# Turning blocks 1 to 7 of the first two x tiles ahead of the first gate product, in a new order of the opening

## The chip, the core and the metric

The kernel runs on one core of a Trainium2 chip. The metric is the device time of one execution in microseconds, lower is better. Before the change three runs gave 669.2, 669.93 and 670.37 us, a median of 669.93 us.

The core's engines each run their own list of instructions in order and meet only at semaphores: TensorE (PE, with weight loads shown as PEld), VectorE (DVE), ScalarE (ACT), GpSimd (POOL) and SyncE (SP, which here only issues DMAs). ScalarE can issue DMAs too, on a queue of its own.

## The reference, cut to what matters

The reference is one step of a hybrid diffusion backbone layer over nine tiles of 128 tokens (one tile of prompt, eight of latent tokens), 1024 features wide. Of it the change touches only the front of the first of these lines:

```
shift, scale, gate = modulation(cond, w_mod, b_mod)          # silu(cond) @ w_mod + b_mod
h = rmsnorm(x, norm_gain) * (1.0 + scale) + shift
q_a, k_a, v_a, g_a, q_b, k_b, v_b, g_b = project(h, w_in)     # columns of one product h @ w_in
o = attention over all keys (group A) and over a band (group B)
y = x + gate * (concat(o_a * silu(g_a), o_b * silu(g_b)) @ w_out)
```

All of it is in float32. The kernel splits each operand of a large product into a high and a low part and makes three products of them (high by high, low by high, high by low).

## The kernel before, in words

The program begins with an *opening* that makes `h`, turned so that features lie on partitions, and beside it the first gate products `g_a` (a product of the 512 columns of `w_in` that make the gates of group A). It ends with the kernel's third piece of tokens, in the loop `gates(W_GA, 0, W_QA, THIRDS[2:])`. The rest of the kernel (the other projections, the attention, the output product) isn't touched by the change.

**The data.** `x` comes in nine tiles `xn0` to `xn8` of 128 tokens by 1024 features (`load_x`, 512 KB each; tile 0 is the prompt and comes last). The modulation weights come in eight pieces `wm0` to `wm7` (`load_wm`, 1 MB each), of which three fit at a time; the gate weights in eight pieces `rawga_0` to `rawga_7` (`W_GA.load`, 256 KB each), of which three fit. A small identity matrix (`ident`, 64 KB) and a table of columns (`colt`, 24 KB: the conditioning vectors, the norm gain, the bias) are loaded first. All of these loads are issued by SP in one queue.

**The steps.** For a feature block `j` (0 to 7), the opening makes these:

- `norm(t)`: for a tile of x, the sum of squares on ScalarE (L594; with `halves` one half of it on VectorE, L597) and the root on GpSimd (L601, L599, L603); `scaled(t)` multiplies the tile by it in place (L587 on VectorE, L585 on ScalarE).
- `modulate_rows(j)`: eight products (shown as sixteen instructions in the trace) of the silu of the condition with `wm[j]` on TensorE (L551, into `pm`), and a copy to `mrows` on VectorE (L556). I call this *rows j*.
- `modulate(j)`: two transposes of `mrows` (L562) and three small instructions on VectorE, which give the scale `a_mod` and the shift `b_col` of block j (L568 to L572).
- `transposed(j, t0, n)`: turns block j of n tiles from t0 on into a PSUM bank `px` on TensorE (L608, one transpose of 128x128 for each tile), applies scale and shift on ScalarE (L617, into `hf`), makes the high part of h on VectorE (L622) and the low part on GpSimd (L623).
- `W_GA.split`: high part of the weights on ScalarE (L435), low part on VectorE (L440), and the load of the next piece on SP.
- `first_half(half, parts)`: the gate products of block 0, for tiles 1 and 2 (half 0) and for tiles 3 and 4 (half 1) apart (L648, 128x256 each). `first_gates(ch, k)`: the products of block k for tiles 1 to 4 (L467, L468, L463, 128x512 each), into four PSUM banks `big`. `next_gates(ch, k)`: those of tiles 5 and 6 (128x256 each), into two banks `small`.
- `warm(n)`: n products of the identity by itself (L631) whose result nobody reads.

**The order.** The order of the opening's instructions on each engine is the order in which the program calls these steps. Before, it stands in a loop over j with a dozen conditions and small tables (`TURNED`, `BEHIND`, `WARM`, `LOADS`, `PAIRED`): 16 warm-up products, rows 0, block 0 of tiles 1 and 2 turned, six more warm-up products around `modulate(0)`, and then the first gate product; from there on four transposes (tiles 1 to 4) for each further block j, just ahead of its gate products. The modulation of blocks 4 and 5 and of 6 and 7 is made in pairs.

PSUM has eight banks: four `big`, two `small`, and two (`D` and `E`) that take turns for `pm` and `px`.

Of the kernel before, what the change touches and what calls it, by code (L numbers as in the profile page):

```python
# [20 lines left out]
P = 128  # L21
# [29 lines left out]
X_FROM = 2  # L51
SECOND_FROM = 5
LOADS = (1, 2, "m", 3, 4, "w", "m", "w", "m", 5, 6)
WARM = (16, 1, 5)
FULL = 1
MROWS_ACT = (7,)
SOON = 8
PAIRED = (4, 6)

TURNED = ((), (), (), (0,), (1, 2), (3,), (4, 5), (6, 7), (), ())  # L60
BEHIND = ((), (), (), (), (0,), (1, 2), (3,), (4, 5), (6,), (7,))
WIDE = 5
# [237 lines left out]
def hybrid_step(ctx, tc, x_prompt, x_sample, cache_k_a, cache_v_a, cache_k_b, cache_v_b,  # L300
# [104 lines left out]
    class Weights:  # L405
# [32 lines left out]
        def low(self, k, h, l):  # L438
            eng = nc.gpsimd if self.tag in POOL_LO and k % 2 else nc.vector
            eng.tensor_tensor(l, self.raw[k], h, op=ALU.subtract)  # L440
            self.hi.append(h)
            self.lo.append(l)
            self.load()
# [73 lines left out]
    with tc.tile_pool(name="st", bufs=2, side="right") as st:  # L517
        ident = st.tile([P, P], F32, name="ident", bufs=1)
        nc.sync.dma_start(ident, k_ident)
# [3 lines left out]
        nc.sync.dma_start(colt, cols)  # L523
        st.tile([P, 16], F32, name="pad3", bufs=1)

        wm = []

# [46 lines left out]
        xn = {}  # L574

        def load_x(t):
            xn[t] = st.tile([P, D], F32, name=f"xn{t}", bufs=1)
# [28 lines left out]
        def turned(px, j, t0, n):  # L606
            for i in range(n):
                nc.tensor.transpose(px[:, P * i : P * i + P], xn[t0 + i][:, P * j : P * j + P], ident)  # L608

        def transposed(j, t0, n, cond, px=None):  # L610
            if px is None:
                px = bank_tr(f"px{j}_{t0}")
                turned(px, j, t0, n)
# [3 lines left out]
            nc.scalar.activation(hf[:, :w], px[:, :w], AF.Identity,  # L617
                                 scale=a_mod[:, j, cond : cond + 1], bias=b_col[:, j, cond : cond + 1])
# [5 lines left out]

        for step in LOADS:
            load_x(step) if step in FIRST else W_GA.load() if step == "w" else load_wm(len(wm))

# [4 lines left out]

        rest = [7, 8, 0]
        second = [(j, 7, 2, 0) for j in range(WIDE)] + [(j, 0, 1, 1) for j in range(KT)]

# [19 lines left out]
        def more():  # L655
            ready = [x for x in second if x[0] <= j]
            if ready and j >= SECOND_FROM:
                second.remove(ready[0])
                transposed(*ready[0])

        for j in range(KT + 2):
            if j == 0:
                for t in (1, 2):
                    norm(t)
                    scaled(t)
                warm(WARM[0])
                modulate_rows(0)
                turned(small[1], 0, 1, 2)
                warm(WARM[1])
                modulate(0)  # L670
                warm(WARM[2])
                norm(3)
                norm(4, True)
                scaled(3, slice(0, 2 * P))
                transposed(0, 1, 2, 0, small[1])
                hi = W_GA.high()
                scaled(4, slice(0, 2 * P), nc.scalar)
                W_GA.low(*hi)
                first_half(0, 0)
                transposed(0, 3, 2, 0)  # L680
                modulate_rows(1)
                first_half(0, 1, 2)
                load_wm(3)
                continue
            if j == 1:
                modulate(1)
                W_GA.split()
                transposed(1, 1, 4, 0)
                first_half(1, 0, 1, 2)
                scaled(3, slice(2 * P, D))  # L690
                scaled(4, slice(2 * P, D), nc.scalar)
                load_wm(4)
                norm(5)
                continue
            big_on, behind = j <= KT, BEHIND[j]
            if SOON <= j < KT:
# [943 lines left out]
```

## Time and profile before

| | before |
|---|---|
| time, median of three runs | 669.93 us |
| the profiled execution's time | 669.37 us |
| span of the profiled execution, first to last instruction | 667.5 us |
| TensorE busy, share of the span | 98% |
| VectorE, ScalarE, GpSimd busy | 66%, 42%, 50% |
| chain of work that ended last: share on TensorE | 92% |
| first gate product starts | 14.78 us |
| product of the opening's last stretch (`pg`, after the last turn) starts | 66.90 us |

The profiled execution took 1.87 us more than its span, and 0.56 us less than the median of the three runs. In the lines of a timeline the columns are the start in us, the length in us, the engine, the source line, the operation, what it writes and reads, its size and how many of them are merged; in brackets is how long the engine had been idle before, and what let it go. In a table of windows each engine has its busy time and its number of instructions; the last three columns are the granted clock of TensorE, the mean busy share of the 16 DMA engines and the GB/s that they moved. A chain is read in order of time: start, length, what it was spent on.

### The profile page before, as it was taken

The numbers are of one execution on the slowest core, as the hardware profiler recorded it, in microseconds if no ns is written. First come the engines' busy times: TensorE is split into PE (matmuls) and PEld (weight loads), VectorE is DVE, ScalarE is ACT, GpSimd is POOL, SyncE is SP. The second block draws the span as 40 slices with busy tenths as digits, with TensorE's granted clock in tenths as the row PEclk, the third lists the DMA queues.
The fourth block names the chain that finished last, engine by engine and source line by source line (L and its number), as shares of the span: only waits on it lengthen the run. The fifth ranks groups of instructions, "written<-read, shape, count | busy, mean of one in ns | idle before, by whom it ended". The sixth has DMA issues, their size and how long they took to land.

```text
span 667.5 us, 10648 instructions
## 1 busy us (share of the span) xinstructions
PE 655.5 (98%) x3757; PEld 517.5 (78%) x3757; DVE 438.6 (66%) x924; ACT 281.3 (42%) x586; POOL 332.3 (50%) x324
## 2 busy tenths in 40 slices
PE   6999999999999999999999999999999999999997
PEld 2789988887788788997777777777777777777766
DVE  3566147786684766446768878688787786875533
ACT  4555411242142453435554355444454355434531
POOL 2457013332321232357885575657665675557712
PEclk9999999999999999999999999999999999999999
DMA  8980365437645211744142302223132212332233
GB/s 323 413 304 6 131 231 151 91 77 224 185 108 146 91 48 37 224 127 148 56 132 100 99 31 97 89 72 96 41 119 88 72 53 83 124 92 78 76 103 111
DMA packets 55837, 81.41 MB, mean 122 GB/s; under 512 B 7388, under 2 KB 26932, under 8 KB 54760
## 3 DMA queue, kind: packets, MB, share of 16 engines
q1 hardware_dynamic: 47752, 69.06, 30.9%
q10 hardware_dynamic: 8032, 11.68, 6.9%
q8 instruction: 30, 0.49, 0.3%
q14 instruction: 23, 0.19, 0.1%
HBM read 61.42 MB, written 19.29 MB: 121 GB/s over the span
## 4 chain that ended last, share of the span: by engine, by line
PE 92%; DVE 2%; ACT 2%; DMA 2%; issue 1%; ACTq 1%; SPq 0%; POOL 0%; DVEq 0%
PE pv L1432 15%; PE po L1507 15%; PE st L1390 7%; PE st L1391 7%; PE pmx L1130 5%; PE pq L454 4%; PE pq L455 4%; PE pq L453 4%; PE pg L468 3%; PE pg L463 3%; PE pg L467 3%; PE pk L454 2%; PE pk L455 2%; PE pk L453 2%; PE pmx L1133 2%; DMA xn<-in_x_sample_dram 1%
## 5 line engine op out<-in xcount | busy, mean ns | idle before, releaser
L1415 POOL TENSOR_TENSOR acc<-acc,pe 128x512 f32<-128x512 f32 x112 | 150.0, 1339 | 6.8 <-ACT pe L1402 0.6
L1402 ACT ACTIVATE pe<-st 128x512 f32<-128x512 f32 x208 | 120.4, 594 | 65.0 <-PE st L1391 52.3
L1143 DVE TENSOR_REDUCE mx<-pmx 128x1 f32<-128x384 f32 x192 | 104.4, 553 | 34.9 <-PE pmx L1130 32.1
L1432 PE MATMUL pv<-pe,v_all 128*64 128x256 f32 x832 | 96.8, 381 | 0.0
L1432 PEld LDWEIGHTS pv<-pe,v_all 128*64 128x64 f32 x832 | 58.3, 137 | 33.0 <-PE st L1391 4.2
L1507 PE MATMUL po<-wo,ogh 128*128 128x512 f32 (+1 forms) x224 | 79.5, 387 | 0.0
L372 POOL TENSOR_TENSOR rs_q<-ms_q,mhalf 128x8 f32<-128x8 f32 x18 | 34.8, 1931 | 80.1 <-DVE ms_q L370 80.1
L1130 PE MATMUL pmx<-kha,qt 128*128 128x384 f32 x192 | 64.1, 347 | 0.0
L1390 PE MATMUL st<-qt,kha 128*128 128x512 f32 x144 | 57.4, 398 | 0.5 <-ACT pe L1402 0.5
L1391 PE MATMUL st<-qb,kla 65*128 65x512 f32 x144 | 57.1, 396 | 0.0
L1148 DVE CUSTOM_DVE_ANT_0 pmx<-pmx,mask,nsink 128x512 f32<-128x512 f32 (+1 forms) x64 | 44.2, 722 | 11.4 <-PE pmx L1133 11.4
L1507 PEld LDWEIGHTS po<-wo,ogh 128*128 128x128 f32 x224 | 41.6, 189 | 9.5 <-ACT ogh L1469 0.6
L1464 POOL TENSOR_TENSOR spare<-spare,sgl 128x256 f32<-128x256 f32 x27 | 19.5, 735 | 50.0 <-DVE spare L1460 47.5
L1130 PEld LDWEIGHTS pmx<-kha,qt 128*128 128x128 f32 x192 | 35.3, 189 | 11.4 <-issue 5.0
L1507 PE MATMUL po<-wo,ogl 128*128 128x512 f32 (+1 forms) x112 | 43.2, 386 | 0.0
L1415 DVE TENSOR_TENSOR acc<-acc,pe 128x512 f32<-128x512 f32 x28 | 34.3, 1226 | 5.2 <-ACT pe L1402 3.9
L623 POOL TENSOR_TENSOR h<-hf,h 128x256 fp32r<-128x256 f32 (+2 forms) x33 | 28.0, 864 | 19.2 <-DVE h L622 19.2
L861 ACT ACTIVATE sqq<-pq 128x512 f32<-128x512 f32 x18 | 10.8, 599 | 53.6 <-DMA qd<-qo0q 15.7
L1390 PEld LDWEIGHTS st<-qt,kha 128*128 128x128 f32 x144 | 27.2, 189 | 5.7 <-ACT pe L1402 1.2
L467 PE MATMUL pg<-h,whigb 128*128 128x512 f32 (+2 forms) x88 | 30.0, 341 | 0.0
L1391 PEld LDWEIGHTS st<-qb,kla 65*128 65x128 f32 x144 | 27.0, 188 | 3.5
L468 PE MATMUL pg<-h,wlogb 128*128 128x512 f32 (+2 forms) x88 | 29.7, 337 | 0.0
(231 smaller groups left out, 1495.4 us busy)
## 6 DMA issues: line engine op xcount, KB each, us to landing
qt<-qd SPq DMA_DIRECT2D x36, 256.0 KB
wm<-in_w_mod_ss_dram SPq DMA_DIRECT2D x8, 1024.0 KB
qd<-qo0q ACTq DMA_DIRECT2D x36, 128.0 KB
qd<-qo1q ACTq DMA_DIRECT2D x36, 128.0 KB
qb<-qd SPq DMA_DIRECT2D x36, 128.0 KB
sgl<-gd SPq DMA_DIRECT2D x36, 128.0 KB
out_dram<-yt SPq DMA_DIRECT2D x17, 256.0 KB
xn<-in_x_sample_dram SPq DMA_DIRECT2D x8, 512.0 KB
```

What stands on the lines that cost most here:

```text
L453: nc.tensor.matmul(out, h_at(0, i, k, tok), w.hi[k], start=(k == 0), stop=False)
L467: nc.tensor.matmul(out, w.hi[k][:, cs], h_at(0, i, k, to), start=(k == 0 and first), stop=False)
L468: nc.tensor.matmul(out, w.lo[k][:, cs], h_at(0, i, k, to), start=False, stop=False)
L1130: nc.tensor.matmul(pm[:, 0:384], lhs, kha[:, g, 3 * b : 3 * b + 3, :], start=True, stop=True)
L1143: nc.vector.tensor_reduce(mx[:, h, b : b + 1], pm[:, 0:384], axis=AX.X, op=ALU.max)
L1148: nc.vector.tensor_tensor_reduce(s, s, mask[:, m0 : m0 + P * (p1_ - p0)], -1.0, nsink[:, 4 * g + h : 4 * g + h + 1], op0=ALU.add, op1=ALU.min,
L1390: nc.tensor.matmul(s, kh, qtile[i], start=True, stop=False)
L1391: nc.tensor.matmul(s, kl, qbtile[i], start=False, stop=True)
L1402: nc.scalar.activation(pe, v["s"], AF.Exp)
L1415: (nc.vector if (m, b) in ADD_DVE else nc.gpsimd).tensor_tensor(acc[i], first, pe, op=ALU.add)
L1432: nc.tensor.matmul(pv[HD * s : HD * s + HD, o : o + 256].rearrange("p (c n) -> p c n", c=2), lhs, r[:, :, s, :], start=start, stop=stop)
L1507: nc.tensor.matmul(po[c], x, wo_parts[KT * n + k][lo][:, q], start=(k == KS[0] and p == 0), stop=(k == KS[-1] and p == 2))
```

## The change

1. The loop over j, its tables and the `LOADS` list are replaced by one written table `OPENING`, a list of steps in the order in which they are called, each of them one of the functions above or a part of one. `W_GA` no longer loads its next piece by itself after a split; the table says when.
2. Tiles 1 to 4 of x lie in one buffer `x14` instead of four buffers of their own. Tile 2 is loaded and normed ahead of tile 1.
3. The loads of `ident` and `colt` are issued on ScalarE's queue instead of SP's.
4. Blocks 1 to 7 of tiles 1 and 2 are turned ahead of the first gate product (`early`, 14 transposes into the four `big` banks, which are empty then) and copied back to their place in `x14` (`kept`: two pairs of blocks on ScalarE, a pair and a single block on VectorE). Later, `turned` leaves these out, and `transposed` applies scale and shift with two instructions of 128x256 on ScalarE, one from `x14`, one from the bank with tiles 3 and 4, where one of 128x512 stood.
5. The warm-up products are 16 at the start and 14 ahead of the first gate product, where 16, 1 and 5 stood.
6. The order of the rest is new too: which gate products stand between which turns, and some of the scaling moves from one engine to another (`scaled(2)` and `scaled(7)` to ScalarE, the first columns of tile 4 to VectorE; tiles 1, 6 and 0 are normed in halves on two engines).

```diff
+OPENING = (('x', 2), ('x', 1), ('wm',), ('x', 3), ('x', 4), ('w',), ('wm',), ('w',), ('norm', 2), ('wm',),
+           ('norm', 1, True), ('scaled', 1, 0, 8, False), ('x', 6), ('warm', 16), ('x', 5),
+           ('scaled', 2, 0, 8, True), ('turn', 0, 1, 2, True), ('early', 1, 3, 2, 1), ('rows', 0),
...
-        nc.sync.dma_start(ident, k_ident)
+        nc.scalar.dma_start(ident, k_ident)
...
-        nc.sync.dma_start(colt, cols)
+        nc.scalar.dma_start(colt, cols)
...
+        x14 = st.tile([P, 4, D], F32, name="x14", bufs=1)
...
-            xn[t] = st.tile([P, D], F32, name=f"xn{t}", bufs=1)
+            xn[t] = x14[:, t - 1] if 1 <= t <= 4 else st.tile([P, D], F32, name=f"xn{t}", bufs=1)
...
             for i in range(n):
+                if (j, t0 + i - (t0 + i + 1) % 2) in own:
+                    continue
                 nc.tensor.transpose(px[:, P * i : P * i + P], xn[t0 + i][:, P * j : P * j + P], ident)
...
-            nc.scalar.activation(hf[:, :w], px[:, :w], AF.Identity,
-                                 scale=a_mod[:, j, cond : cond + 1], bias=b_col[:, j, cond : cond + 1])
+            for i in range(0, n, 2 if (j, t0) in own or (j, t0 + 2) in own else n):
+                at = slice(P * i, w if n < 2 or (j, t0) not in own and (j, t0 + 2) not in own else P * i + 2 * P)
+                if (j, t0 + i) in own:
+                    out = hf[:, at].rearrange("p (t c) -> p t c", c=P)
+                    x = x14[:, t0 + i - 1 : t0 + i + 1, P * j : P * j + P]
+                else:
+                    out, x = hf[:, at], px[:, at]
+                nc.scalar.activation(out, x, AF.Identity,
+                                     scale=a_mod[:, j, cond : cond + 1], bias=b_col[:, j, cond : cond + 1])
...
+        def early(b, j0, n, t0):
+            at[b] = big[b] if b < 4 else small[0] if b == 4 else bank_tr(f"pe{b}")
+            for i in range(n):
+                for k in range(2):
+                    nc.tensor.transpose(at[b][:, P * (2 * i + k) : P * (2 * i + k) + P],
+                                        xn[t0 + k][:, P * (j0 + i) : P * (j0 + i) + P], ident)
+
+        def kept(b, j0, n, t0, on_act=False):
+            (nc.scalar.copy if on_act else nc.vector.tensor_copy)(
+                x14[:, t0 - 1 : t0 + 1, P * j0 : P * (j0 + n)].rearrange("p t (j c) -> p j t c", c=P),
+                at[b][:, 0 : 2 * P * n].rearrange("p (j t c) -> p j t c", t=2, c=P))
+            own.update((j0 + i, t0) for i in range(n))
...
+        for name, *args in OPENING:
+            act[name](*args)
```

What this does to the order on the engines is shown at three places. Names carry a running number at their end; `x14` is the buffer of tiles 1 to 4, `pg0_1_f` to `pg0_3_f` are `big` banks.

SP's queue at the start of the program, before (the loads of `ident` and `colt`, then tiles 1 and 2, then the modulation weights):

```order
L519 DMA ident_163<-in_k_ident_dram 128x128
L523 DMA colt_167<-in_cols_dram 128x48
L578 DMA xn1_177<-in_x_sample_dram 128x1024
L578 DMA xn2_179<-in_x_sample_dram 128x1024
L530 DMA wm0_181<-in_w_mod_ss_dram 128x2048
L578 DMA xn3_183<-in_x_sample_dram 128x1024
```

and after:

```order
L616 DMA x14_177<-in_x_sample_dram 128x1024 x2
L567 DMA wm0_186<-in_w_mod_ss_dram 128x2048
L616 DMA x14_177<-in_x_sample_dram 128x1024 x2
L450 DMA rawga_0_190<-in_w_in_dram 128x512
L567 DMA wm1_192<-in_w_mod_ss_dram 128x2048
```

The two small loads no longer stand ahead of the first tile in SP's queue; the rest of this queue keeps nearly its order (tile 6 ahead of tile 5, two gate pieces a place earlier). ScalarE's list at the same place, before (the sums of squares L594 of tiles 1 to 4, then scale and shift L617 of block 0, then the high part of the first weights L435):

```order
L594 ACTIVATE sq1_205,ss1_206<-xn1_177 128x1024
L594 ACTIVATE sq2_213,ss2_214<-xn2_179 128x1024
L594 ACTIVATE sq3_262,ss3_263<-xn3_183 128x1024
L594 ACTIVATE sq4_269,ss4_270<-xn4_185 128x512
L617 ACTIVATE hf0_1_278<-pg0_2_s_204,b_col_151,a_mod_150 128x256
L435 CAST whiga_0_282<-rawga_0_187 128x512
```

and after:

```order
L632 ACTIVATE sq2_196,ss2_197<-x14_177 128x1024
L632 ACTIVATE sq1_205,ss1_206<-x14_177 128x512
L623 ACTIVATE x14_177<-x14_177,rsx2_201 128x1024
L718 COPY x14_177<-pg0_1_f_179 128x2x2x128
L718 COPY x14_177<-pg0_2_f_180 128x2x2x128
L632 ACTIVATE sq3_272,ss3_273<-x14_177 128x1024
L632 ACTIVATE sq4_279,ss4_280<-x14_177 128x512
L661 ACTIVATE hf0_1_301<-pg0_2_s_183,b_col_151,a_mod_150 128x256
L465 CAST whiga_0_305<-rawga_0_190 128x512
```

Three instructions now stand between the sums of squares of the first two tiles and that of tile 3: the scaling of tile 2 and two of the four copies back. TensorE's list from rows 0 on, before (rows 0 is `pm0<-wm0`; `px` and `pg0_2_s` take turned blocks):

```order
L551 MATMUL pm0_237<-wm0_181,sil32_174 32x256 x8
L608 MATMUL pg0_2_s_204<-ident_163,xn1_177 128x128
L608 MATMUL pg0_2_s_204<-ident_163,xn2_179 128x128
L631 LDWEIGHTS ident_b_103
L631 MATMUL pg0_0_s_203<-ident_b_103 128x512
L562 MATMUL pm0_237<-ident_163,mrows0_246 128x128 x2
```

and after, from the end of the first 16 warm-up products on:

```order
L648 MATMUL pg0_2_s_183<-ident_163,x14_177 128x128 x2
L714 MATMUL pg0_1_f_179<-ident_163,x14_177 128x128 x4
L588 MATMUL pm0_241<-wm0_186,sil32_174 32x256 x8
L714 MATMUL pg0_0_f_178<-ident_163,x14_177 128x128 x4
L714 MATMUL pg0_2_f_180<-ident_163,x14_177 128x128 x4
L714 MATMUL pg0_3_f_181<-ident_163,x14_177 128x128 x2
L599 MATMUL pm0_241<-ident_163,mrows0_250 128x128 x2
```

Six transposes (two of them those of block 0) now stand ahead of rows 0, ten more stand between rows 0 and the two transposes of `modulate(0)`, and 14 warm-up products follow those where five stood. For a later block j, here block 2, TensorE's list had four transposes before:

```order
L562 MATMUL pm2_365<-ident_163,mrows2_374 128x128 x2
L608 MATMUL px2_1_396<-ident_163,xn1_177 128x128
L608 MATMUL px2_1_396<-ident_163,xn2_179 128x128
L608 MATMUL px2_1_396<-ident_163,xn3_183 128x128
L608 MATMUL px2_1_396<-ident_163,xn4_185 128x128
L463 MATMUL pg0_0_f_199<-h1_0_1_126,whiga_1_327 128x512
```

and now has two, behind the products of one more gate chunk:

```order
L599 MATMUL pm2_366<-ident_163,mrows2_375 128x128 x2
L498 MATMUL pg0_2_f_180<-h0_0_1_118,whiga_1_356 128x512
L499 MATMUL pg0_2_f_180<-h0_0_1_118,wloga_1_357 128x512
L494 MATMUL pg0_2_f_180<-h1_0_1_126,whiga_1_356 128x512
L648 MATMUL px2_1_419<-ident_163,x14_177 128x128 x2
L494 MATMUL pg0_0_f_178<-h1_0_1_126,whiga_1_356 128x512
```

The two transposes of tiles 1 and 2 are gone from this place, and from the same place of every block from 1 to 7.

More of the change, by code (lines that the diff above doesn't have):

```diff
@@ L442, in low @@
             self.lo.append(l)
-            self.load()
+            if self.tag != "ga":
+                self.load()
     W_QA = Weights([(CQ[0], 512)], "qa")
@@ new lines, in hybrid_step @@
+        parts = []
+        def early(b, j0, n, t0):
[9 more added lines that the diff above has]
+            own.update((j0 + i, t0) for i in range(n))
```

179 lines of the change are left out of this document (65 added, 114 removed).

## The prediction

> **What bounds the kernel now.** I read the page's head and its chain first, to see whose time the span is.
>
> ```profile
> span 667.5 us, 10648 instructions
> PE 92%; DVE 2%; ACT 2%; DMA 2%; issue 1%; ACTq 1%; SPq 0%; POOL 0%; DVEq 0%
> ```
>
> TensorE carries the chain, so the opening's time shifts all behind it one for one. Next, the windows of the opening: from the first gate product to the end of rows 5, and from there to the last turn.
>
> ```profile
> 14.70:32.30 17.60, 16.92 (x151) 12.16 (x151) 9.34 (x24) 8.73 (x14) 8.58 (x11) 1.00 1.03 416
> 32.30:66.90 34.60, 34.45 (x250) 30.06 (x251) 22.84 (x49) 19.03 (x35) 22.59 (x32) 1.00 0.43 162
> ```
>
> In the first stretch the DMA engines are full (share 1.03, 416 GB/s); in the second they aren't, and TensorE is busy 34.45 of 34.60 us. So there are two regimes, and the timeline shows what ends the waits in the first:
>
> ```profile
> 22.32 0.62 ACT L435 CAST whiga<-rawga 128x512 fp32r<-128x512 f32 x1 [0.44 <-DMA rawga<-in_w_in_dram]
> 25.49 1.07 PE L551 MATMUL pm<-wm,sil 128*32 128x256 f32 x16 [0.50 <-DVE xn L587]
> 26.03 0.62 ACT L435 CAST whiga<-rawga 128x512 fp32r<-128x512 f32 x1 [0.74 <-DMA rawga<-in_w_in_dram]
> 30.34 1.93 PE L551 MATMUL pm<-wm,sil 128*32 128x256 f32 x32
> 32.38 1.06 ACT L594 ACTIVATE sq<-xn 128x1024 bf16<-128x1024 f32 x1 [1.31 <-DMA xn<-in_x_sample_dram]
> ```
>
> Gate piece 3 has landed at 26.0 us, tile 7 at 32.35. In SP's queue `wm3` stands just ahead of that piece (256 KB, 0.63 us at 416 GB/s) and `wm5` just ahead of tile 7 (512 KB, 1.26 us). So `wm3` landed at about 25.4 and `wm5` at about 31.1. Rows 3 started at 25.49; I put its wait down to `wm3`, not to VectorE's scaling, since nothing in rows 3 reads that tile. Rows 4 and 5 are one group of 1.93 us from 30.34 on; rows 5, its second half, started at 31.3, just after `wm5`. Until 31.3 the opening is paced by the loads; behind it TensorE is full.
>
> **The change part by part.** All sums are against the profiled execution (669.37 us, 0.56 under the median of the three runs).
>
> *A. The fourteen transposes.* Their price and that of the products around them, from the chain of waits:
>
> ```profile
> 38.95 0.44 PE px L608 x4
> 39.38 0.46 PE pg_f L463 x2
> ```
>
> That is 0.11 us for a transpose, 0.23 for a 128x512 product. Of the fourteen, the two each of blocks 4 to 7 stood behind rows 5, where TensorE is full: 8 x 0.11 = 0.87 us, a gain with nothing to hide it. The six of blocks 1 to 3 (0.65 us) stood in the stretch that the loads pace; they only give slack to step B.
>
> *B. The loads start earlier.* SP issued `ident` at 0.74 and the first x tile at 1.66 us:
>
> ```profile
> 0.74 0.40 SPq L519 DMA_DIRECT2D ident<-in_k_ident_dram  x1
> 1.66 0.90 SPq L578 DMA_DIRECT2D xn<-in_x_sample_dram  x2
> ```
>
> With the two small loads on ScalarE's queue, tile 2 goes out at 0.74, all of the queue 0.92 us sooner. What the engines did then, us by us:
>
> ```profile
> 1.00:2.00 1.00, 0.00 (x0) 0.00 (x0) 0.00 (x0) 1.00 (x1) 0.04 (x1) 1.00 0.15 46
> 2.00:3.00 1.00, 0.03 (x1) 0.04 (x2) 0.36 (x2) 0.02 (x1) 0.00 (x0) 1.00 0.20 45
> 3.00:4.00 1.00, 1.00 (x3) 0.40 (x4) 0.35 (x2) 0.21 (x1) 0.00 (x0) 1.00 0.94 360
> ```
>
> From 3 us on they are full; ahead of it the small loads took 0.15 + 0.20 = 0.35 us of them. If tile 2 comes at the same time, that work is in its way: the loads gain between 0.92 - 0.35 = 0.57 and 0.92 us. I take 0.75, the middle. The Trainium skill says in "DMA: Bandwidth & Descriptors", section "Issuing engines are not separate DMA queues", that loads issued by several engines run on the same 16 engines and interleave; by it alone only the lower end is due. `wm5` then lands at 30.3 instead of 31.1.
>
> *C. Can TensorE follow?* The path to the first gate product, before:
>
> ```profile
> 2.97 6.08 PE L631 MATMUL pg_s<-ident_b 128*128 128x512 bf16 x16 [2.97 <-DVE ident_b L521]
> 10.31 1.07 PE L551 MATMUL pm<-wm,sil 128*32 128x256 f32 x16 [1.27 <-DMA wm<-in_w_mod_ss_dram]
> 11.55 1.06 ACT L594 ACTIVATE sq<-xn 128x1024 bf16<-128x1024 f32 x1 [3.57 <-DMA xn<-in_x_sample_dram]
> 12.20 1.24 PE L631 MATMUL pg_s<-ident_b 128*128 128x512 bf16 x5
> 12.86 0.63 ACT L594 ACTIVATE sq<-xn 128x512 bf16<-128x512 f32 x1 [0.15 <-DMA xn<-in_x_sample_dram]
> 13.49 0.55 ACT L617 ACTIVATE hf<-pg_s,b_col,a_mod 128x256 f32<-128x256 f32 x1
> 13.94 0.60 ACT L435 CAST whiga<-rawga 128x512 fp32r<-128x512 f32 x1
> 14.78 0.72 PE L648 MATMUL pg_f<-h,whiga 128*128 128x256 f32 x4 [1.34 <-DVE h L622]
> ```
>
> ScalarE runs straight from tile 3's sum of squares at 11.55 to the product at 14.78: 3.2 us. Now its second copy back stands ahead of that sum, and waits for TensorE: warm-up to 9.05, six transposes to 9.7 (0.65), rows 0 from about 9.8 to 10.9 (`wm0`, at 10.3 before, is there at 9.55), eight transposes to 11.8, one copy of 128x512, for which I take ScalarE's 0.78 us for that size out of PSUM, less the 0.1 us by which neighbours overlap:
>
> ```profile
> 19.24 0.78 ACT L617 ACTIVATE hf<-px,b_col,a_mod 128x512 f32<-128x512 f32 x1 [2.04 <-DVE b_col L572]
> ```
>
> So the sum starts at about 12.5 and the first gate product at 12.5 + 3.2 = 15.7, some 0.9 us *later* than before. The 14 warm-up products (14 x 0.25 = 3.5 us, from the five in 1.24) end at 15.6 if `modulate(0)`'s transposes are done at 12.1, and cover that wait. `modulate(0)` itself waits on VectorE behind two copies back (to about 13.6 instead of 13.03), still ahead of ScalarE's need at 14.5.
>
> Before, TensorE needed 25.49 - 14.78 = 10.7 us from there to rows 3. What it had to do: 24 products of 128x256, rows 1 and 2, and the turns of block 1; the chain gives
>
> ```profile
> 18.47 0.44 PE px L608 x4
> 18.91 1.43 PE pg_f L648 x12
> 20.34 1.00 PE pm L551 x16
> ```
>
> so 2.86 + 2.0, four transposes of `modulate` 0.44, ten of x 1.09, twelve products of block 1 2.77: 9.2 us of work and 1.5 of waits. After the change four of the ten transposes are gone: 8.7 of work. Rows 2 now comes ahead of twelve products that need nothing new, which covers the chain from rows 1 through block 1's `h`. I allow 0.5 us of waits (the scaling of tiles 3 and 4 for the first turn, the copy of `mrows2` behind VectorE's other work). Rows 3 then starts at 15.7 + 9.2 = 24.9, with `wm3` there at 24.65, and rows 5 at 24.9 + 5.4 = 30.3 (rows 3 1.0, twelve products of block 2 2.77, six transposes 0.65 for `modulate(3)`, block 3 and block 0 of tiles 5 and 6, rows 4 0.96), the moment `wm5` lands. So rows 5 starts 1.0 us sooner than at 31.3, TensorE and the loads arriving together.
>
> *D. Behind rows 5.* The work shrinks by A's 0.87. ScalarE gets more: two instructions of 128x256 for one of 128x512,
>
> ```profile
> 36.47 1.02 ACT L617 ACTIVATE hf<-px,b_col,a_mod 128x256 f32<-128x256 f32 x2 [1.05 <-PE px L608]
> 35.90 0.75 DVE L587 TENSOR_SCALAR xn<-xn,rsx 128x1024 f32<-128x1024 f32 x1
> 40.79 1.85 DVE L587 TENSOR_SCALAR xn<-xn,rsx 128x1024 f32<-128x1024 f32 x1
> 42.73 0.38 PE L608 MATMUL px<-ident,xn 128*128 128x128 f32 x2
> ```
>
> 0.24 us for each of the blocks 4 to 7, and the scaling of tile 7; in a stretch where it is busy 19.03 of 34.60 us, that lies beside TensorE's work. One place is tight: tile 8 is scaled at 40.79 (1.85 us; alone it takes 0.75) and turned at 42.73. Now TensorE comes there at about 40.6, and the scaling, behind tile 8's norm and block 5's parts, is done at 40.7 to 41.8. I allow 0.25 us for this and for block 4's low part. At the end before, the eight single turns of tile 0 stood close together, behind one another through two banks, and the chain left TensorE:
>
> ```profile
> 65.04 0.43 ACT hf L617
> 65.47 0.41 issue
> 65.87 0.47 ACT hf L617
> 66.39 0.33 PE px L608
> ```
>
> Products kept it busy but for about 0.3 us before 66.39. In the new list these turns have up to eleven products between them, so this goes. Zero cost: the shared buffer `x14` (same bytes, and each load still releases its own tile), fewer instructions on none of the bounds, later loads (tile 8 keeps its place, the last gate pieces come sooner).
>
> **Sum:** -1.0 (rows 5) - 0.87 (eight transposes) - 0.3 (end) + 0.25 (new waits) = -1.9 us: 667.5 against the profiled execution, 668.0 against the median of 669.93. 0.2%, 1.34 us, is about what a measurement of this kernel can tell from no change, so faster begins at 668.6.
>
> **The rivals.**
> *R1, ScalarE's lateness isn't made good.* Each wait above my 0.5 us ahead of rows 3 or 0.25 behind rows 5 goes straight into the sum. For it: the first product is 0.9 us later, and the list has no slack at `wm3`; the tile 8 place alone can cost 1.2. Against: rows 2 and twelve products of block 0 now stand where TensorE used to wait for block 1. With 1.4 us of waits more: 669.4, no change that can be told.
> *R2, the loads don't come sooner* (the small loads and tile 2 share the engines, or the start is set by something else). Then rows 5 keeps 31.1: -0.2 - 0.87 - 0.3 + 0.25 = -1.1: 668.8.
> *R3, slower: the clock falls.* The first warm-up products ran at half pace,
>
> ```profile
> 3.80 0.15 PEld L631 LDWEIGHTS <-ident_b 128*128 128x128 bf16 x1 [0.28 <-issue]
> 4.23 0.15 PEld L631 LDWEIGHTS <-ident_b 128*128 128x128 bf16 x1 [0.28 <-issue]
> ```
>
> 0.43 us apart, against 0.25 for the five at 12.20. If the 1.8 us of transposes around rows 0 let TensorE fall back, 14 products take 14 x 0.43 = 6.0 us instead of 3.5: the first gate product comes 2.5 us later, and the first twelve of them (0.12 us each) cost 1.4 more. Then rows 5 starts near 34, 2.9 late instead of 1.0 early: +2.9 - 0.87 - 0.3 + 0.25 = +2.0: 671.9. It decides once the fall costs over about 3.3 us of the path. Against it: before, TensorE stood 1.2 us idle ahead of rows 0 and was fast after it, and later
>
> ```profile
> 56.06 1.03 PE L608 MATMUL px<-ident,xn 128*128 128x128 f32 x8
> ```
>
> eight transposes in one piece left the pace as it was. The Trainium skill says in "TensorE: Matmul & The Clock Gate", section "Part 4: PE-mode transpose", that a transpose does not count as busy time for the clock in the way that a product does, which would speak for this rival; fourteen around rows 0, right after the slow start, are not in any row of before.
>
> **How the numbers follow.** Forecast 0.58, R1 0.18, R2 0.15, R3 0.09. Of the forecast's cases (its own range 667.1 to 668.7) nearly all are faster by over 0.2%, and a third of R2's: 0.56 + 0.05 = 0.61. R1, the rest of R2 and a little of the forecast are no change: 0.31. R3 makes 0.08 slower. The range leaves out R3 and a little below: its low end adds 1.0 us of gain to the forecast (no new waits at all, loads 0.92 sooner, and half a us between measurements), its high end takes in R1: 667.0 to 669.9.
>
> **What would show it.** Right: the first gate product at 15 to 16 us, *later* than 14.78, with the warm-up products ending just ahead of it; tile 2 landing near 4.4; rows 3 near 24.9 and rows 5 near 30.3; the stretch from rows 5 to the first `pg` product 34.7 us instead of 35.6, with under 0.5 us idle. Wrong: rows 3 later than 25.5 (R1), gate piece 3 still at 26.0 (R2), products of 128x512 0.43 us apart after 9 us (R3), or a TensorE wait at tile 8's turn of over a us.

## The result, and the profile after

The changed kernel took 672.58 us (median of 4 runs, 672.32 to 672.77) against 669.57 for the kernel before (4 runs, 668.87 to 670.37). The ratio is 1.0051, with a 95% interval of 1.004 to 1.0063: slower by 3.0 us, where 1.9 us less was forecast. Here and in the table of the experiments a ratio need not be that of the two medians, since a few runs at a lower granted clock (0.997 in five of E2's eleven, 0.949 in one of E13's) count in it too.

The timeline of the kernel after, at the places that the prediction names (start, duration, engine, line, what; in brackets the idle time before it and what ended it):

```profile
4.83 0.23 DVE L551 CAST ident_r<-ident 128x128 fp32r<-128x128 f32 x1 [3.96 <-DMA ident<-in_k_ident_dram]
5.25 5.56 PE L672 MATMUL pg_s<-ident_b 128*128 128x512 bf16 x16 [5.25 <-DVE ident_b L552]
6.19 0.22 ACT L570 ACTIVATE silc<-colt 128x16 f32<-128x16 f32 x1 [3.25 <-DMA colt<-in_cols_dram]
6.31 1.04 ACT L632 ACTIVATE sq<-x 128x1024 bf16<-128x1024 f32 x1
13.80 3.19 PE L672 MATMUL pg_s<-ident_b 128*128 128x512 bf16 x14
17.01 0.74 PE L686 MATMUL pg_f<-h,whiga 128*128 128x256 f32 x4
18.72 0.44 PE L648 MATMUL px<-ident,x 128*128 128x128 f32 x2 [0.97 <-DVE x L625]
27.62 0.61 ACT L465 CAST whiga<-rawga 128x512 fp32r<-128x512 f32 x1
27.86 1.07 PE L588 MATMUL pm<-wm,sil 128*32 128x256 f32 x16
28.14 1.76 DVE L635 CUSTOM_DVE_ANT_0 sq<-xn 128x512 bf16<-128x512 f32 x1
30.31 0.44 PE L599 MATMUL pm<-ident,mrows 128*128 128x128 f32 x2 [0.24 <-DVE mrows L593]
33.53 1.93 PE L588 MATMUL pm<-wm,sil 128*32 128x256 f32 x32 [0.45 <-ACT hf L661]
45.90 0.33 PE L648 MATMUL px<-ident,xn 128*128 128x128 f32 x1 [0.89 <-DVE xn L625]
69.91 0.34 PE L498 MATMUL pg<-h,whiga 128*128 128x384 f32 x1
```

The first gate product comes at 17.01 instead of 14.78, rows 3 at 27.86 instead of 25.49, rows 5 (second half of the group at 33.53) at 34.50 instead of 31.30, and the first `pg` product of the next stage at 69.91 instead of 66.90. By 34.50 the kernel is 3.20 us late, of which 0.19 is won back behind. Gate piece 3, which ScalarE waited for until 26.03 before, is split at 27.62 without a wait. So it had landed by then, but no row tells when: the prediction's sign for R2 can't be read in this kernel (E2 gives it).

The same stretches as windows (length, then busy time of PE, PEld, DVE, ACT, POOL, the granted clock, the DMA share, GB/s), first of the kernel before, then of the kernel after: first product to rows 1, to rows 3, to rows 5, to the first `pg` product.

```profile
14.78:16.03 1.25, 1.15 (x6) 0.76 (x7) 0.48 (x1) 0.54 (x2) 1.07 (x2) 1.00 1.09 441
16.03:25.49 9.46, 8.95 (x77) 6.81 (x78) 5.56 (x15) 6.23 (x10) 3.78 (x5) 1.00 1.02 411
25.49:31.30 5.81, 5.81 (x56) 4.14 (x60) 2.90 (x8) 1.96 (x3) 2.88 (x4) 1.00 1.02 415
31.30:66.90 35.60, 35.44 (x270) 30.48 (x263) 23.16 (x50) 19.03 (x35) 23.36 (x33) 1.00 0.45 170
```

```profile
17.01:19.57 2.56, 1.59 (x11) 1.25 (x11) 1.67 (x3) 0.38 (x1) 1.24 (x2) 1.00 1.01 402
19.57:27.86 8.29, 8.24 (x69) 5.68 (x68) 5.11 (x15) 5.94 (x13) 3.81 (x5) 1.00 1.03 420
27.86:34.50 6.64, 5.95 (x55) 3.60 (x58) 4.96 (x11) 2.45 (x5) 2.80 (x4) 1.00 0.93 359
34.50:69.91 35.41, 34.52 (x262) 29.50 (x255) 21.94 (x51) 20.09 (x41) 24.19 (x34) 1.00 0.36 128
```

Read two columns: length and PE's busy time. Before, TensorE was busy 1.15 + 8.95 + 5.81 = 15.91 of the 16.52 us ahead of rows 5, so it waited only 0.61 us there (0.50 of it at rows 3, the row at 25.49 in the prediction) although the DMA share stood at 1.02. After, it does 15.78 us of work in 17.49. Behind rows 5 the work fell by 0.92, from 35.44 to 34.52, but the stretch by only 0.19, for a wait of 0.89 at tile 8's turn came in.

SP's queue, where it issues modulation pieces 4 and 5 (one group of two), in the kernel before and in the kernel after:

```profile
17.16 4.58 SPq L530 DMA_DIRECT2D wm<-in_w_mod_ss_dram  x2
20.70 2.65 SPq L567 DMA_DIRECT2D wm<-in_w_mod_ss_dram  x2
```

Three pieces fit at a time, and piece 4 goes out as soon as rows 1 are done with theirs, before (16.03 + 1.07 = 17.10) and after (19.57 + 1.07 = 20.64). From there on the issue of the loads follows TensorE, and not the start of the queue.

### The profile page after: what moved, and what is told of

The parts are those of the page before. It is cut to its first block, busy times and chain, and to the rows that moved or that the text cites. A ratio compares the mean times of both kernels' runs of the same rounds, so it can differ in the third digit from the quotient of the medians.

```text
span 670.5 us, 10678 instructions
## 1 busy us (share of the span) xinstructions
PE 657.0 (98%) x3765; PEld 517.5 (77%) x3765; DVE 440.3 (66%) x931; ACT 283.9 (42%) x596; POOL 333.3 (50%) x324
## 4 chain that ended last, share of the span: by engine, by line
PE 89%; DVE 3%; ACT 2%; issue 1%; POOL 1%; ACTq 1%; DMA 0%; DVEq 0%; POOLq 0%
PE pv L1416 15%; PE po L1491 15%; PE st L1374 7%; PE st L1375 7%; PE pmx L1114 5%; PE pq L485 4%; PE pq L486 4%; PE pq L484 4%; PE pg L499 3%; PE pg L498 3%; PE pg L494 3%; PE pk L485 2%; PE pk L486 2%; PE pk L484 2%; PE pmx L1117 2%
```

## The experiments

Fourteen kernels ran. Times are medians in us, each with the kernel before on the same chip.

| kernel | time | before | ratio, 95% interval |
|---|---|---|---|
| after | 672.58 | 669.57 | 1.0051, 1.004 to 1.0063 |
| e1_small_on_sp | 671.54 | 669.41 | 1.0031, 1.002 to 1.0043 |
| e2_before_small_on_act | 669.34 | 669.41 | 1.0012, 1.0 to 1.0025 |
| e3_only_colt_on_act | 671.69 | 669.41 | 1.003, 1.0018 to 1.0041 |
| e4_wm_first | 673.57 (one run) | 669.41 | none |
| e5_norm6_whole | 670.79 | 669.27 | 1.0025, 1.0015 to 1.0034 |
| e6_norm3_first | 671.03 | 669.27 | 1.0026, 1.0016 to 1.0036 |
| e7_scale_4_on_act | 671.34 | 669.27 | 1.0034, 1.0022 to 1.0046 |
| e8_no_early | 669.96 | 669.27 | 1.0011, 1.0002 to 1.0019 |
| e9_scale_8_on_act | 670.66 | 669.07 | 1.0022, 1.0014 to 1.0031 |
| e10_all | 669.44 | 669.07 | 1.0003, 0.9995 to 1.0012 |
| e11_no_early_all | 668.53 | 669.07 | 0.9995, 0.9986 to 1.0004 |
| e12_mod_first | 668.88 | 669.14 | 0.9996, 0.9987 to 1.0005 |
| e13_warm_9 | 668.59 | 669.22 | 0.9999, 0.9981 to 1.0016 |
| e14_norm4_whole | 668.48 | 669.22 | 0.9988, 0.9979 to 0.9997 |

**E1, the small loads back on SP's queue**, all else as after:

```diff
-        nc.scalar.dma_start(ident, k_ident)
+        nc.sync.dma_start(ident, k_ident)
...
-        nc.scalar.dma_start(colt, cols)
+        nc.sync.dma_start(colt, cols)
```

> The changed kernel with the loads of ident and colt back on SP, ahead of tile 2. Theory T1 (on ScalarE's queue the two small loads take turns with the first large tiles and land with them, so warm-up products and the first sum of squares start 2.2 us late, and the new order has no slack for it): ident lands at 2.5 us, warm-up products start at 3.0, the first gate product at 15.4 to 15.9 instead of 17.0, the kernel is 2 to 4 us faster than the changed one, 668.5 to 669.5. Rival T3 (the transposes and copies ahead of the first product, and the new order behind it, are the loss, wherever the small loads are): first product at 16.5 or later, 671 or more.

The timeline of this kernel:

```profile
2.68 0.23 DVE L551 CAST ident_r<-ident 128x128 fp32r<-128x128 f32 x1 [1.81 <-DMA ident<-in_k_ident_dram]
5.11 1.06 ACT L632 ACTIVATE sq<-x 128x1024 bf16<-128x1024 f32 x1 [1.92 <-DMA x<-in_x_sample_dram]
15.97 0.74 PE L686 MATMUL pg_f<-h,whiga 128*128 128x256 f32 x4
```

`ident` is there at 2.68 instead of 4.83, the first sum of squares starts at 5.11, when its tile lands, instead of 6.31 behind `silc`, and the first gate product comes 1.04 us sooner. The median falls by 1.04 too (by 0.88, if each kernel is set against the kernel before on its own chip: 3.01 and 2.13 us slower). So the move to ScalarE's queue cost about 1 us. T1 has the path nearly right, but not the time: 2.1 us of loss is elsewhere, and 671.54 is what T3 gave.

**E2, the kernel before with its two small loads on ScalarE's queue** (the same two lines, the other way round).

> The kernel before with only the loads of ident and colt moved to ScalarE's queue. T1: ident lands at 4.6 to 5.0 us and colt near 6, as in the changed kernel; the old order reads the tiles' sums later and turns nothing ahead of rows 0, so its first product comes at 14.9 to 15.3 (0.2 to 0.5 late), while the large loads come 0.9 us sooner; 668.6 to 669.8. T1b (the late small loads cost their 2.2 us in any order): 671.5. T3: the small loads are harmless, large loads sooner: 668.6 or less.

```profile
4.83 0.23 DVE L520 CAST ident_r<-ident 128x128 fp32r<-128x128 f32 x1 [3.95 <-DMA ident<-in_k_ident_dram]
14.54 0.74 PE L648 MATMUL pg_f<-h,whiga 128*128 128x256 f32 x4 [0.80 <-ACT whiga L435]
16.21 0.33 PE L608 MATMUL px<-ident,xn 128*128 128x128 f32 x1 [0.82 <-ACT xn L585]
25.37 1.07 PE L551 MATMUL pm<-wm,sil 128*32 128x256 f32 x16
25.92 0.62 ACT L435 CAST whiga<-rawga 128x512 fp32r<-128x512 f32 x1 [0.20 <-DMA rawga<-in_w_in_dram]
```

They come just as late. In the old order the first gate product isn't later for it (14.54 against 14.78; T1 had said 14.9 to 15.3), but the turn behind it is: it waits 0.82 us for a tile's scaling, and rows 1 start at 16.46 instead of 16.03. At rows 3 that is made good (25.37 against 25.49), for the 0.50 us that the kernel before waits there is gone. So this order has slack where the new one has none. The medians are 0.07 us apart; the interval reaches up to 1.0025, so a small cost isn't ruled out. As to the large loads, SP issues the first tile at 0.74 here and not at 1.66. Tile 3's sum of squares can start 1.06 us sooner (10.49 against 11.55), but gate piece 3 is there at 25.92 instead of 26.03: of the 0.92 us, 0.11 is left by then.

**E3, only `colt` on ScalarE's queue**, `ident` on SP's:

```diff
-        nc.scalar.dma_start(ident, k_ident)
+        nc.sync.dma_start(ident, k_ident)
```

> The changed kernel with ident back on SP and colt alone on ScalarE's queue. T1: warm-up products start at 3.0; colt (eight packets for each DMA engine, each behind one packet of tile 2) lands at 3.7 to 4.6, ahead of or with tile 2, and costs nothing; first product 15.4 to 15.9, large loads 0.45 us sooner than before; 668.0 to 669.2, not slower than with both on SP. T2 (ScalarE's queue is late by itself, whatever SP carries): colt lands at 5.0 or later, the sum of squares of tile 2 starts at 5.3 or later, first product 16.2 or later. T3: 671 or more.

```profile
2.87 0.22 ACT L570 ACTIVATE silc<-colt 128x16 f32<-128x16 f32 x1 [0.40 <-DMA colt<-in_cols_dram]
```

Here `colt` is early too (2.87), since it goes out on its own queue beside `ident`, ahead of the tiles; the time, 671.69, is E1's within its spread (T1's 668.0 to 669.2 left out the loss that is elsewhere). The queue alone does no harm; a large load in flight beside the small one does.

**E4, the 1 MB modulation piece ahead of tile 2** in SP's queue, small loads on ScalarE's, to see what the small load waits for:

```diff
-OPENING = (('x', 2), ('x', 1), ('wm',), ('x', 3), ...
+OPENING = (('wm',), ('x', 2), ('x', 1), ('x', 3), ...
```

> The changed kernel with the first modulation piece (8 KB packets) ahead of tiles 2 and 1 (4 KB packets) in SP's queue; made to read when ident lands, not to be fast. T1: ident's packets now alternate with packets that take twice as long, so it lands at 5.5 to 6.2 instead of 4.8, and the warm-up products start at 6.0 to 6.7. T2 (ScalarE's queue has a fixed delay): ident lands at 4.6 to 5.0 as before, warm-up products at 5.2.

```profile
6.08 0.23 DVE L551 CAST ident_r<-ident 128x128 fp32r<-128x128 f32 x1 [5.20 <-DMA ident<-in_k_ident_dram]
```

Issued at the same time (0.74), `ident` lands at 6.08 beside a load with 8 KB in each partition, at 4.83 beside one with 4 KB, at 2.68 ahead of all. The delay grows with the load beside it, so it isn't a fixed price of ScalarE's queue. (That load is also the larger one, 1 MB against 512 KB; E4 doesn't tell the two apart.) The Trainium skill says in "DMA: Bandwidth & Descriptors", section "Queues, rings and completion order", that each engine goes in turn through the queues it has work for, a packet at a time; the three landings agree with that. No run here shows the single turns.

**E5 to E9** are E1 with one more edit each. They ran on other chips than E1, so each is read by what it lies over the kernel before on its own chip: E1 2.13 us, E5 1.52, E6 1.76, E7 2.07, E8 0.69, E9 1.59. (The expectations were written against E1's 671.54.) The intervals reach some 0.6 us or more to each side, so of these only E8's time by itself is apart from E1's; for the others the timelines carry the reading. E5, tile 6's sum of squares whole on ScalarE:

```diff
-('norm', 6, True)
+('norm', 6)
```

> The changed kernel with both small loads back on SP's queue (671.54 us), and tile 6's sum of squares made whole on ScalarE, as before, instead of half on VectorE. Theory L (the loss is a sum of late links in the new order, one of them tile 6's half sum on VectorE, 1.76 to 1.78 us long beside GpSimd): mod 3's wait of 0.24 to 0.27 goes, rows 4 start 0.6 to 1.0 us sooner after rows 3 (5.68 us apart now, 4.85 before the change), and the time falls to 670.5 to 671.0. Rival P (the early transposes and their copies cost as much as they save, and the waits seen are only where that shows): the next wait takes this one's place, and the time stays within 0.2 us of 671.54.

```profile
27.05 1.07 PE L588 MATMUL pm<-wm,sil 128*32 128x256 f32 x16
28.18 0.42 DVE L593 COPY mrows<-pm 128x256 f32<-128x256 f32 x1 [0.77 <-PE pm L588]
31.99 1.93 PE L588 MATMUL pm<-wm,sil 128*32 128x256 f32 x32 [0.24 <-ACT hf L661]
```

The copy of `mrows3` now follows rows 3 at once instead of behind the 1.76 us half sum; rows 4 start 4.94 us after rows 3 (5.67 in the kernel after), and the time falls by 0.61. As theory L had it. E6, tile 3's sum of squares ahead of the second copy back:

```diff
-('mod', 0), ('kept', 2, 5, 2, 1, True), ('norm', 3),
+('mod', 0), ('norm', 3), ('kept', 2, 5, 2, 1, True),
```

> The changed kernel with both small loads on SP's queue, and tile 3's sum of squares moved ahead of ScalarE's second copy back. ScalarE was idle 1.40 us ahead of that copy while tile 3 lay landed, so the sum fits there. Theory L: the first hf starts 0.4 to 0.6 us sooner, the first gate product at 15.4 to 15.6 instead of 15.97, the scaling of tiles 3 and 4 with it, and the time falls by 0.4 to 0.7 to 670.8 to 671.1. Rival P: first product as said, but the turn of tiles 3 and 4 and what follows take the gain back, time within 0.2 us of 671.54.

```profile
14.64 0.56 ACT L661 ACTIVATE hf<-pg_s,b_col,a_mod 128x256 f32<-128x256 f32 x1 [0.66 <-DVE b_col L609]
15.85 0.82 PE L686 MATMUL pg_f<-h,whiga 128*128 128x256 f32 x4
```

The sum starts at 11.28, and now ScalarE waits for VectorE's columns (0.66), which stand behind two copies back: a new last link. The first product comes only 0.12 us sooner than in E1, where L said 0.4 to 0.6; this execution's first transposes start 0.26 later (9.84 against 9.58), so that 0.38 is the fairer figure. The time falls by 0.37, a little less than L's 0.4 to 0.7. E7, tile 4's first scaling on ScalarE:

```diff
-('high',), ('scaled', 4, 0, 2, False),
+('high',), ('scaled', 4, 0, 2, True),
```

> The changed kernel with both small loads on SP's queue, and tile 4's first scaling on ScalarE, beside tile 3's on VectorE, instead of both on VectorE (1.07 us for the two). Theory L: the wait ahead of the turn of tiles 3 and 4 (0.97) falls to 0.3 to 0.6, and the time by 0.4 to 0.6 to 670.9 to 671.1. Rival P: wait shorter, time within 0.2 us of 671.54.

```profile
17.33 0.33 PE L648 MATMUL px<-ident,x 128*128 128x128 f32 x1 [0.34 <-ACT x L623]
```

The wait falls from 0.97 (in E1 as in the kernel after) to 0.34, and from the first product to rows 1 it is 2.10 us instead of E1's 2.54. But the time falls only by 0.06, where L said 0.4 to 0.6: nothing that can be told. E8, no early transposes and no copies back, 6 warm-up products for 14:

```diff
-('early', 1, 3, 2, 1), ('rows', 0), ('early', 0, 1, 2, 1), ('early', 2, 5, 2, 1), ('early', 3, 7, 1, 1),
-('kept', 1, 3, 2, 1, True), ('kept', 3, 7, 1, 1, False), ('kept', 0, 1, 2, 1, False), ('mod', 0),
-('kept', 2, 5, 2, 1, True), ('norm', 3), ('norm', 4, True), ('warm', 14),
+('rows', 0), ('mod', 0), ('norm', 3), ('norm', 4, True), ('warm', 6),
```

> The changed kernel with both small loads on SP's queue, and without the early transposes and their copies back: each block of the first two tiles is turned in its own place, as before, with 6 warm-up products instead of 14. Theory L says that the early turns cost more at the start (copies on ScalarE and VectorE ahead of tiles 3 and 4) than they save behind rows 5 (0.87): the first product comes at 14.4 to 14.9 instead of 15.97, tile 8's and tile 6's late links stay, and the time is 670.4 to 671.0. Rival E (the early turns are a gain of about 0.9 and the reordering around them is the whole loss): 672.0 to 672.5.

```profile
10.53 1.06 ACT L630 ACTIVATE sq<-x 128x1024 bf16<-128x1024 f32 x1 [1.41 <-DMA x<-in_x_sample_dram]
14.00 0.74 PE L684 MATMUL pg_f<-h,whiga 128*128 128x256 f32 x4 [0.59 <-ACT whiga L463]
```

The first gate product comes at 14.00, 1.97 us sooner than in E1, and the time falls by 1.44, more than the 0.5 to 1.1 that L had said. The window behind rows 5 shows what is given up:

```profile
31.48:67.34 35.86, 35.40 (x270) 30.42 (x263) 21.35 (x51) 19.70 (x37) 24.13 (x34) 1.00 0.42 158
```

That is 35.40 us of TensorE work instead of 34.52. The stretch itself is only 0.45 longer than in the kernel after (35.86 against 35.41), for the wait at tile 8's turn is shorter too. In this order the early transposes save 0.88 us of work and make the first product 1.97 late. E9, tile 8's scaling on ScalarE:

```diff
-('scaled', 8, 0, 8, False)
+('scaled', 8, 0, 8, True)
```

> The changed kernel with both small loads on SP's queue (671.54 us), and tile 8's scaling on ScalarE (about 1.05 us) instead of VectorE, where it took 1.84 beside GpSimd. Theory L: the wait ahead of tile 8's first turn (0.93) falls to 0.2 to 0.5, and the time by 0.3 to 0.6 to 670.9 to 671.2. Rival P: the hf of block 3 that stands behind the scaling on ScalarE comes 1.1 us later, TensorE waits for it instead, and the time stays within 0.2 us of 671.54.

```profile
44.54 0.33 PE L648 MATMUL px<-ident,xn 128*128 128x128 f32 x1 [0.20 <-ACT xn L623]
```

The wait of 0.93 (E1) falls to 0.20, and the time by 0.54, in L's 0.3 to 0.6.

**E10, all of E5, E6, E7 and E9 together**, early transposes kept (the four edits above).

> The early transposes kept, and every late link mended at once: both small loads on SP's queue, tile 3's sum ahead of ScalarE's second copy, tile 4's first scaling and tile 8's on ScalarE, tile 6's sum whole. Theory L, if the links add: 671.54 less 0.51, 0.20, 0.75 and 0.3 to 0.5 is 669.4 to 669.9, about the time before the change. Rival P: the links stand beside each other, not one behind the other, and the time stays above 670.4.

```profile
32.42:67.18 34.76, 34.56 (x262) 29.50 (x255) 20.88 (x50) 21.81 (x42) 24.25 (x34) 1.00 0.40 153
```

669.44, 0.37 over the kernel before, no difference that can be told. That is 1.76 less than E1, and the four steps by themselves add up to 1.58: the links add, since each stood on TensorE's path at another time. The window is that behind rows 5. With tile 8's wait down to 0.2 it is 0.84 us shorter than before the change (34.76 against 35.60). E11, the same order with each block turned in its own place, takes 35.26 there, so 0.50 of that comes from the early transposes.

**E11, the same without the early transposes** (E8's edit, and E5's, E7's and E9's).

> The same mended order without the early transposes and their copies (each block turned in its own place, 6 warm-up products instead of 14). The kernel without early transposes alone took 669.96. Theory L: less 0.75 for tile 6's sum, 0.2 to 0.5 for tile 4's scaling and 0 to 0.4 for tile 8's, this is 668.3 to 669.0, faster than before the change by 0.3 to 1.0 us; the early transposes then cost 0.5 to 1.5 us net even in an order that is mended for them. Rival E (once the late links are gone, the early transposes save the 0.87 us that they take out behind rows 5): this one is slower than the mended order with early transposes, by 0.3 to 0.9 us.

668.53 on the same chip, 0.91 less than E10. In that order, too, the early transposes cost more than they save. Its profiled execution shows a new wait:

```profile
11.49 1.06 ACT L630 ACTIVATE sq<-x 128x1024 bf16<-128x1024 f32 x1 [2.73 <-DMA x<-in_x_sample_dram]
26.22 1.07 PE L586 MATMUL pm<-wm,sil 128*32 128x256 f32 x16 [0.95 <-DMA wm<-in_w_mod_ss_dram]
```

Here a load does end a wait of TensorE, at rows 3. This execution took 669.51 us, 0.98 over E11's median, which is about that wait; no trace shows it for the other runs.

**E12, block 0's modulation after 8 early transposes instead of 14**, its columns behind one copy back instead of two, and ScalarE's second copy back behind tile 4's sum of squares; otherwise E10:

```diff
-('early', 2, 5, 2, 1), ('early', 3, 7, 1, 1), ('kept', 1, 3, 2, 1, True), ('kept', 3, 7, 1, 1, False),
-('kept', 0, 1, 2, 1, False), ('mod', 0), ('norm', 3), ('kept', 2, 5, 2, 1, True), ('norm', 4, True),
+('kept', 1, 3, 2, 1, True), ('kept', 0, 1, 2, 1, False), ('mod', 0), ('early', 2, 5, 2, 1),
+('early', 3, 7, 1, 1), ('kept', 3, 7, 1, 1, False), ('norm', 3), ('norm', 4, True), ('kept', 2, 5, 2, 1, True),
```

> The mended order with early transposes (669.44 us), with block 0's modulation turned after the first 8 early transposes instead of after all 14, and its columns on VectorE behind one of its two copies back instead of both. Theory L (the early transposes cost at the start because their transposes and copies stand ahead of the chain that ends in the first gate product: mrows 12.16, mod 12.75, columns 13.94 to 14.56, hf 14.60, product 15.80): columns done at 13.3 to 13.5, first product at 15.0 to 15.3, time 0.4 to 0.7 us under the mended order, 668.7 to 669.1, still not under the order without early transposes (668.53). Rival E (their cost at the start was only this order): first product at 14.5 or before, time 668.4 or less.

```profile
14.22 0.29 DVE L666 CAST h<-hf 128x256 fp32r<-128x256 f32 x1
15.77 0.82 PE L686 MATMUL pg_f<-h,whiga 128*128 128x256 f32 x4
16.08 0.51 ACT L623 ACTIVATE x<-x,rsx 128x256 f32<-128x256 f32 x1 [1.51 <-POOL rsx L641]
```

The time is L's, the way to it isn't: `h` is there at 14.51, but the product stays at 15.77, held by the 14 warm-up products (E13 shows it). The gain came from the turn of tiles 3 and 4: tile 4's scaling starts at 16.08 instead of 16.83 in E10, and rows 1 at 17.48 instead of 18.22.

**E13, 9 warm-up products instead of 14 in E12**, and **E14, 11 of them and tile 4's sum of squares whole on ScalarE** (E14's edit against E12):

```diff
-('norm', 4, True), ('kept', 2, 5, 2, 1, True), ('warm', 14),
+('norm', 4), ('kept', 2, 5, 2, 1, True), ('warm', 11),
```

> The kernel before it (modulation first, 668.88 us) with 9 warm-up products ahead of the first gate product instead of 14: 14 of them start at 12.94 and hold TensorE until 15.77, while h and the weight piece are ready at 14.57; 9 end at about 15.0. Theory W (the count of warm-up products holds the opening): first gate product at 14.6 to 15.0, rows 1 sooner by 0.5 us or more, time 668.1 to 668.4. Theory T4 (tile 4's scaling, at 16.08 to 16.6, ends last there): first product as said, rows 1 sooner by under 0.2, time 668.6 to 668.9.

> Modulation first, 11 warm-up products, and tile 4's sum of squares whole on ScalarE instead of half on VectorE, where it stands behind block 0's columns and a copy back and ends at 14.2. ScalarE: whole sum 12.4 to 13.7, copy back 14.2, hf 14.75, weight piece 15.3; first product at 15.3. Tile 4's root at 14.5 to 14.8 instead of 16.05, its scaling behind the weight piece at 15.3 to 15.9. Theory T4: turn of tiles 3 and 4 at 16.0 to 16.2 instead of 16.65, rows 1 at 16.8 to 17.1 instead of 17.48, time 668.2 to 668.6. Theory W: rows 1 as in the run with 9 warm-up products, time no lower than that one's.

E13's timeline, then E14's:

```profile
14.71 0.82 PE L686 MATMUL pg_f<-h,whiga 128*128 128x256 f32 x4
16.66 0.33 PE L648 MATMUL px<-ident,x 128*128 128x128 f32 x1 [1.03 <-ACT x L623]
17.48 1.07 PE L588 MATMUL pm<-wm,sil 128*32 128x256 f32 x16
```

```profile
15.52 0.75 PE L686 MATMUL pg_f<-h,whiga 128*128 128x256 f32 x4
16.89 1.07 PE L588 MATMUL pm<-wm,sil 128*32 128x256 f32 x16
```

In E13 the first product comes a microsecond sooner and rows 1 at 17.48 as before: the microsecond becomes a wait (1.03) for tile 4. In E14 the first product is later than in E13 and rows 1 sooner, by 0.59. So tile 4's scaling ended last, not the warm-up products. E14's interval lies below 1: with the early transposes, it is faster than the kernel before by 0.03 to 0.21%; as the only such interval among fourteen that is weak evidence. E11, without them, ran on another chip with an overlapping interval; which of the two orders is the better stays open.

## Why the prediction was wrong

- **What bounds the kernel: the failed step.** "Until 31.3 the opening is paced by the loads" didn't hold, and with it went the term of -1.0 us for rows 5. A DMA share of 1.03 says that the engines are full, not that TensorE waits for them. The row quoted in the prediction had TensorE busy 16.92 of 17.60 us; between the first product and rows 5 it had 15.91 us of work and 0.61 of waits. So earlier loads had 0.61 us to give at most. Less the six transposes (0.65) the work is 15.26 (the kernel after has 15.78): from a first product at 15.7, rows 5 could come at 30.96 at best, never at 30.3. Nor do the loads come 0.92 sooner by then: in E2 gate piece 3 gains 0.11, and from modulation piece 4 on SP can issue a load only when TensorE's rows free a buffer. Of the kernels after the change, only E11's profiled execution shows TensorE waiting for a load between the first product and rows 5.
- **A, eight transposes less behind rows 5: right.** 0.87 forecast; TensorE's work there fell by 0.92 (35.44 to 34.52), and E8 gives 0.88 back. In time it is less: with the wait at tile 8's turn down to 0.2, E10's stretch is 0.50 shorter than E11's (34.76 and 35.26).
- **B, the small loads on ScalarE's queue: wrong.** They were taken to share the engines for 0.35 us. `ident` landed 2.15 us later than in E1, so that the warm-up products held TensorE until the first transposes at 10.65; `colt` held `silc` and the first sum of squares to 6.31, and with it the scaling of tile 1 to 10.56. The two chains end within 0.1 us of each other, and together they cost 1.04 us (E1). The rule cited there, that loads of several engines interleave, held; what I didn't ask of it is what interleaving does to the small one.
- **C, the path to the first product: right; what follows, mis-sized.** 15.7 forecast, 15.97 in E1, where the small loads are early. From there to rows 3 it allowed 8.7 us of work and 0.5 of waits: the windows show 1.59 + 8.24 = 9.83 of work and 1.02 of waits, 0.97 of them at the turn of tiles 3 and 4. From rows 3 to rows 5, 5.4 was allowed: 5.95 of work, and 0.69 of waits (0.24 + 0.45), of which 0.24 stays when tile 6's half sum is taken off VectorE (E5); the prediction doesn't mention that sum. Together rows 5 is 4.2 late: 1.3 by the first product, 1.7 by work counted short by per-instruction durations (1.13 + 0.55), 1.2 by waits. The work before the change had been counted short in the same way (9.2, where the windows show 10.10), and the difference was taken for waits that could be won. Part of it is that a product costs more right behind work of another kind: in the kernel after, the first 128x512 product behind rows 3 (28.86) starts 0.34 us ahead of the next one, the two behind it 0.24 and 0.23, and the prediction priced them all at 0.23.
- **D, behind rows 5: two terms wrong.** The 0.25 us for tile 8's turn was 0.89 (E9 shows that it is the scaling on VectorE). The 0.3 us at the end couldn't be had: the whole stretch held 35.60 - 35.44 = 0.16 us of idle time.
- **The rivals.** R1 had the mechanism, lateness that isn't made good, but priced it at 1.4 us of waits and took the loads' gain as given. R2 had the loads right, as far as E2 shows it for the order before (gate piece 3 at 25.92, its sign was "still at 26.0"), but it kept rows 5 at 31.1 and so gave 668.8. R3 didn't happen: the 14 warm-up products took 3.19 us, 0.23 each, after all the transposes. The Trainium skill's rule that was weighed there ("TensorE: Matmul & The Clock Gate", section "Part 4: PE-mode transpose") shows no cost in these rows.

## What to carry to other kernels

Before giving a gain to earlier loads, take the bounding engine's idle time in that stretch: it is all that they can give back. Work moved ahead of the first product pays only if the chain to that product doesn't run through the engines that do the copies; look at what each of its steps is queued behind. A small load that others wait for goes ahead of the large ones, or it shares their pace.

## What the runs showed of the hardware

VectorE and GpSimd hold each other up. Rows of the kernel after, in order of time:

```profile
27.48 0.75 DVE L625 TENSOR_SCALAR xn<-xn,rsx 128x1024 f32<-128x1024 f32 x1
27.64 1.72 POOL L667 TENSOR_TENSOR h<-hf,h 128x512 fp32r<-128x512 f32 x1 [0.69 <-DVE h L666]
44.00 1.84 DVE L625 TENSOR_SCALAR xn<-xn,rsx 128x1024 f32<-128x1024 f32 x1
44.01 1.29 POOL L667 TENSOR_TENSOR h<-hf,h 128x512 fp32r<-128x512 f32 x1
```

At 27.48 VectorE is first: its scaling takes 0.75 and GpSimd's subtraction 1.72. At 44.00 they start within 0.01 us of each other, and it is the other way: GpSimd takes 1.29, and the same scaling 1.84, ending 0.54 us after GpSimd. The half sum at 28.14 (1.76) also ends 0.54 us after the subtraction beside it, at 29.90 against 29.36. The Trainium skill says in "SBUF — State Buffer", section "SBUF: two separate sides", that the two share a pair of ports by a lock that one holds for its whole instruction; these rows agree with it.

The pace of the loads differs between executions: with the same order of loads, tile 3's sum of squares could start at 10.53 in E8's profiled execution and at 11.49 in E11's, the one that took 0.98 us over its median.
